# Forgetting attention's scores: two heads in the two halves of the array's rows, three products each, one worker for both heads

## The chip, the cores and the metric

The kernel runs on one core of a Trainium2 chip. Its engines are TensorE (matrix products; the profile writes PE, and PEld for its weight loads), VectorE (DVE), ScalarE (ACT), GpSimd (POOL) and SyncE (SP, which issues most transfers). The metric is the device time of one execution in microseconds (us).

## The reference, cut to what matters

One layer of a hybrid encoder block on 1024 frames of width 1024: a combined projection feeds eight retention heads and eight forgetting-attention heads of 64 each; then an output projection, cross attention to 256 memory tokens, and a SwiGLU. All in fp32. The part that changes is the scores of the forgetting attention:

```python
fq = rmsnorm(fq.reshape(B, T, N_FOX_HEADS, HEAD_DIM), g_fox_q[l])
fk = rmsnorm(fk.reshape(B, T, N_FOX_HEADS, HEAD_DIM), g_fox_k[l])
...
F = jnp.cumsum(log_f, axis=1).transpose(0, 2, 1)
qh = (q * (d ** -0.5)).transpose(0, 2, 1, 3)
for blk in range(T // Q_BLOCK):
    logits = jnp.einsum('bhqd,bhkd->bhqk', qh[:, :, q0:kend], kh[:, :, :kend])
    logits = logits + F[:, :, q0:kend, None] - F[:, :, None, :kend]
    logits = jnp.where(causal, logits, NEG_INF)
    p = jax.nn.softmax(logits, axis=-1)
    outs.append(jnp.einsum('bhqk,bhkd->bhqd', p, vh[:, :, :kend]))
```

## The kernel before

Every fp32 product is made of products of parts: an operand is split into a high part in fp32r (a reduced fp32 form that the array takes in one pass) and the remainder as a low part. The projections take three products (high by high, high by low, low by high).

The mixing stage goes through eight chunks of projection columns, four pairs of heads p = 0 to 3, retention and attention in turn: r0, f0, r1, f1, r2, f2, r3, f3. Then come the memory's keys and values (`kv_main`), W_out (`wout_main`), and the rest of the layer, which the change does not touch.

**The order.** TensorE's instruction order is written by a planner, class `Driver`. Each piece of work is a generator. It yields either a condition, or a pair (cost, delay): the cost moves the planner's clock `now` on, and the generator is not called again until `now` has passed the delay times `slow` (SLOW = 2.0 in the mixing stage, 1.8 from chunk r3's end on). Spawned generators go ahead of the main line; the main line (the projections) goes on where none is ready; if nothing is ready, the clock moves on with no instruction put down. The clock exists only while the kernel is written: on the chip TensorE takes the instructions in the order put down and waits at each for what it needs. `take_s` and `take_tp` reserve one of three `ps_s` banks or one of two `ps_tp` banks of PSUM for a planned while, `hold` times 1.5.

**The attention of a pair** (`fox_main`) waits until `fox_left` is 0, that is, until the workers of the pair before have finished; its tiles `kst`, `vst` and `fb` have one buffer each. The main line then makes eight projections of 384 columns, two a group, and for each of four groups g (two query tiles of 128 frames) spawns `prep`: three transposes a tile into a `ps_tp` bank, then evictions that leave the queries' high part twice over (128 rows: `qa`) and low part twice over (`qb`), and the keys' high part in rows 0 to 63 and low part in rows 64 to 127 of `kst`, for each head. So a product of 128 rows of `qa` with `kst` holds high by high and high by low at once, and `qb` with `kst` adds low by high and low by low.

Two workers, one a head, go through the groups in `fox_group`:
- scores: for each query tile n = 2g + i + 1 blocks of 128 keys in one or two pieces (`S_CUTS`), a piece being two products into one `ps_s` bank (L642, L643); VectorE adds the forget bias and keeps a running minimum while it reads the bank (L654); ScalarE takes the exponent with a row sum (L661) and scales by the reciprocal (L663), into `s_sb`, of which there are four buffers, two a worker;
- a pause (L665);
- values, for one worker at a time (token `pv`): transposes of `s_sb` in blocks of four into `ps_tp`, split into `p_hi` (ScalarE, L684) and `p_lo` (VectorE, L685), then four products with `vst` a block (L695, L696), and at the end, after the output is copied, a pause of 1200 ns times `slow` (L713).

The retention's scores (`ret_tile`, L463) are products of 64 rows, one head in rows 0 to 63, the other in 64 to 127, each written to its own bank, in plain fp32, which takes two instructions a product. `wout_main` starts when `h` exists, which `fox_end` makes once `fox_left` is 0 after the last pair.

Of the kernel before, what the change touches and what calls it, by code (L numbers as in the profile page):

```python
# [11 lines left out]
F32 = mybir.dt.float32  # L12
# [7 lines left out]
P = 128  # L20
D = 1024
T = 1024
# [131 lines left out]
def trace(tc, a, out):  # L154
# [463 lines left out]

    f_ready = [False]
    S_CUTS = {1: [1], 2: [2], 3: [3], 4: [4], 5: [3, 2], 6: [3, 3], 7: [4, 3], 8: [4, 4]}  # L620
    tok = {"s_sb": 2, "pv": 1}

    def fox_group(p, g, h, qa, qb, kst, vst, fb):

        yield lambda: tok["s_sb"] > 0
        tok["s_sb"] -= 1
        ptiles = []
        for i in range(2):
            qt = 2 * g + i
            n = qt + 1  # L630
            s_sb = foxp.tile([P, T], F32, name="s_sb", tag="s_sb", bufs=4)
            fd = foxp.tile([P, P], F32, name="fd", tag="fd", bufs=2)
            pol.affine_select(fd, fb[:, h, qt * P:(qt + 1) * P], [[-1, P]], ALU.is_ge, 1.0e30, base=0, channel_multiplier=1)
            mins = sm.tile([P, 4], F32, name="mins", tag="mins")
            nm = 0
            b0 = 0
            for nb in S_CUTS[n]:
                w = nb * P
                yield from take_s(1800)
                sps = ps_s()  # L640
                ks = kst[:, h, b0 * P:b0 * P + w]
                mm.matmul(sps[:, :w], qa[:, i, h, :], ks, start=True, stop=False)  # L642
                mm.matmul(sps[:, :w], qb[:, i, h, :], ks, start=False, stop=True)  # L643


                parts = []
                if b0 + nb == n:
                    if nb > 1:
                        parts.append((0, w - P, fb[:, h, b0 * P:b0 * P + w - P]))
                    parts.append((w - P, w, fd))  # L650
                else:
                    parts.append((0, w, fb[:, h, b0 * P:b0 * P + w]))
                for c0, c1, bias in parts:
                    dve.tensor_tensor_reduce(s_sb[:, b0 * P + c0:b0 * P + c1], sps[:, c0:c1], bias, 1.0,  # L654
                                             BIG if nm == 0 else mins[:, nm - 1:nm], ALU.add, ALU.min, mins[:, nm:nm + 1])
                    nm += 1
                b0 += nb
                yield 2 * max(w, 256) / 2.4, 0.0
            sums = sm.tile([P, 2], F32, name="sums", tag="sums")
            with prio(P_EXP):  # L660
                act.activation(s_sb[:, :n * P], s_sb[:, :n * P], AF.Exp, bias=mins[:, nm - 1:nm], scale=-1.0, accum_out=sums[:, 0:1])  # L661
                dve.reciprocal(sums[:, 1:2], sums[:, 0:1])
                act.activation(s_sb[:, :n * P], s_sb[:, :n * P], AF.Identity, scale=sums[:, 1:2])  # L663
            ptiles.append(s_sb)
# [24 lines left out]
        def products():  # L689
            jb, ph, pl, nu, at = blocks.pop(0)  # L690
            yield lambda: drv.now >= at
            for j, u0, cols in ((jb, 0, slice(0, 256)), (jb + 1, 2, slice(0, 256) if nu == 4 else slice(P, 256))):
                u1 = min(u0 + 2, nu)
                last = j == nj - 1
                mm.matmul(pv[:, cols], vst[:, h, j, :], ph[:, u0:u1, :], start=j == 0, stop=False, skip_group_check=True)  # L695
                mm.matmul(pv[:, cols], vst[:, h, j, :], pl[:, u0:u1, :], start=False, stop=last, skip_group_check=True)  # L696
            yield 4 * TR, 0.0

        for jb in range(0, nj, 2):
            yield from transposes(jb)  # L700
            if len(blocks) == 2:
                yield from products()
        tok["s_sb"] += 1
# [15 lines left out]
    def fox_main(c, p):  # L719
        w = weights.pop(c)  # L720
        yield lambda: fox_left[0] == 0
        fox_left[0] = 2
# [12 lines left out]
        drv.spawn(load_fb())  # L735
        parts = {}

        def worker(h):
            for g in range(NG):
                yield lambda: g in parts and fb_loaded[0]  # L740
                yield from fox_group(p, g, h, *parts[g], kst, vst, fb)
            fox_left[0] -= 1

        def prep(g, dups):
            yield 0.0, PREP
            qa = foxp.tile([P, 2, 2, P], F32R, name="qa", tag="qa", bufs=2)
            qb = foxp.tile([P, 2, 2, P], F32R, name="qb", tag="qb", bufs=2)
            for i in range(2):
                t = 2 * g + i
                yield from take_tp(2200)  # L750
                tp = ps_tp()
                for j in range(3):
                    flip(tp[:, j, :], dups[i][:, 2 * j:2 * j + 2, :].rearrange("p b d -> p (b d)"))
                cols = slice(t * P, (t + 1) * P)
                act.activation(qa[:, i], tp[:, 0:2, :], AF.Identity, scale=gqk[:, 0:1])
                for h in range(2):
                    r = slice(h * HD, (h + 1) * HD)
                    act.activation(kst[:HD, h, cols], tp[r, 2, :], AF.Identity, scale=gqk[r, 1:2])
                dve.scalar_tensor_tensor(qb[:, i], tp[:, 0:2, :], gqk[:, 0:1], f32(qa[:, i]), ALU.mult, ALU.subtract)
                for h in range(2):  # L760
                    r = slice(h * HD, (h + 1) * HD)
                    dve.scalar_tensor_tensor(kst[HD:, h, cols], tp[r, 2, :], gqk[r, 1:2], f32(kst[:HD, h, cols]), ALU.mult, ALU.subtract)
                yield 3 * TR, 0.0
            yield 0.0, 1600.0 + SLACK
            parts[g] = (qa, qb)

        drv.spawn(worker(0))
        drv.spawn(worker(1))
        for g in range(NG):
            fqk = foxp.tile([P, 2, 256], F32, name="fqk", tag="fqk", bufs=1)  # L770
            for i in range(2):
# [14 lines left out]
                load_chunk(c + 1)  # L786
            with prio(P_FQK):
                ss = sm.tile([P, 8], F32, name="ss8", tag="ss8")
                dups = [foxp.tile([P, 6, HD], F32, name="dup", tag="dup", bufs=2) for _ in range(2)]
                for i in range(2):  # L790
                    sq = dups[i][:, :4, :]
                    act.activation(sq.rearrange("p a d -> p (a d)"), fqk[:, i, :], AF.Square)
                    dve.tensor_reduce(ss[:, 4 * i:4 * i + 4], sq, AX.X, ALU.add)
                r = rstd(ss, 8, 1.0 / HD)
                for i in range(2):

                    x = fqk[:, i, :].rearrange("p (a d) -> p a d", d=HD)
                    q, k = r[:, 4 * i:4 * i + 2], r[:, 4 * i + 2:4 * i + 4]
                    pol.tensor_tensor(dups[i][:, :4, :].rearrange("p (a b) d -> p a b d", b=2), x[:, :2].unsqueeze(2).to_broadcast([P, 2, 2, HD]),
                                      q.unsqueeze(2).unsqueeze(3).to_broadcast([P, 2, 2, HD]), ALU.mult)  # L800
# [652 lines left out]
```

## Time and profile before

| | |
|---|---|
| time, median of three runs | 1608.91 us (1605.29 to 1613.33) |
| profiled execution, its time | 1609.22 us |
| its span, first to last instruction | 1607.5 us |
| TensorE busy in the span | 97% |
| VectorE, ScalarE, GpSimd busy | 62%, 47%, 10% |
| mean granted TensorE clock | 0.987 of 2.4 GHz |

A busy share is an average over the whole span. Durations of matrix products overlap, since the next one starts before the last has left the array: how fast they follow each other is read from one start to the next. The granted clock is the one that the chip gave TensorE, 1.0 for 2.4 GHz and 0.5 for 1.2.

### The profile page before, as it was taken

Reading aid. Unit: us, or ns where it says so; the run is one execution under the profiler, and the core shown is the slowest. Engines: PE = TensorE matmul, PEld = TensorE weight load, DVE = VectorE, ACT = ScalarE, POOL = GpSimd, SP = SyncE. Lnnn points to the kernel's source line nnn. Section 1 sums busy time; section 2 is a strip of 40 time slices with the busy share of each in tenths; the row PEclk is TensorE's granted clock in tenths of the full one; section 3 lists DMA queues with packets and bytes.
Section 4 is the critical chain, followed back from the end, with each engine's and each line's share of the span. In section 5 each row is a group of like instructions: output and inputs, shape, how many; then the busy total and the mean of one; then the engine's idle time right before and its main releaser. Section 6 shows DMA issues by size and latency. Waiting matters only on the chain.

```text
span 1607.5 us, 21839 instructions
## 1 busy us (share of the span) xinstructions
PE 1552.7 (97%) x7960; PEld 1311.5 (82%) x7960; DVE 995.0 (62%) x2050; ACT 751.8 (47%) x1621; POOL 155.2 (10%) x318
## 2 busy tenths in 40 slices
PE   7999999999999999999989969999999999899998
PEld 6997897898898878888878857888888888688887
DVE  6667657657668943455554567555555554599994
ACT  5457566557658841355554344333333333234231
POOL 0332222232232000000000000000000000000000
PEclk9999999999999999999999989999999999999999
DMA  7031121121133471200343404222222222571202
GB/s 227 6 89 47 35 64 47 35 61 49 35 103 100 137 239 53 79 1 33 104 140 105 119 27 121 89 79 79 79 80 79 79 79 85 217 273 61 96 0 106
DMA packets 142798, 142.15 MB, mean 88 GB/s; under 512 B 9049, under 2 KB 110681, under 8 KB 142178
## 3 DMA queue, kind: packets, MB, share of 16 engines
q1 hardware_dynamic: 138370, 125.02, 25.2%
q0 software_dynamic: 4320, 15.73, 2.5%
q8 instruction: 63, 1.03, 0.3%
q14 instruction: 45, 0.37, 0.1%
HBM read 112.38 MB, written 28.34 MB: 88 GB/s over the span
## 4 chain that ended last, share of the span: by engine, by line
PE 85%; DVE 5%; ACT 5%; DMA 2%; issue 2%; POOL 1%; SPq 0%; POOLq 0%; DVEq 0%; ACTq 0%
PE ps_mm L270 10%; PE ps_mm L271 10%; PE ps_mm L272 10%; PE ps_s L1167 7%; PE ps_s L1169 7%; PE ps_s L1168 7%; PE ps_tp L175 5%; PE ps_tp L1167 4%; PE ps_tp L1168 4%; PE ps_tp L1169 4%; PE ps_mm L1168 2%; PE ps_mm L1169 2%; PE ps_mm L1167 2%; PE ps_pv L696 1%; PE ps_s L270 1%
## 5 line engine op out<-in xcount | busy, mean ns | idle before, releaser
L270 PE MATMUL ps_mm<-w_hi,cv_hi 128*128 128x512 f32 x384 | 156.0, 406 | 6.3 <-ACT qsq L1081 3.3
L272 PE MATMUL ps_mm<-w_hi,cv_lo 128*128 128x512 f32 x384 | 152.3, 397 | 0.0
L271 PE MATMUL ps_mm<-w_lo,cv_hi 128*128 128x512 f32 x384 | 152.1, 396 | 0.0
L1332 ACT CAST op<-raw_d 128x2048 fp32r<-128x2048 f32 (+1 forms) x42 | 72.7, 1764 | 126.5 <-issue 50.8
L1290 ACT CAST w_hi<-t 128x512 fp32r<-128x512 f32 x88 | 54.2, 621 | 160.2 <-PE ps_tp L1168 71.8
L240 DVE TENSOR_TENSOR w_lo<-raw,w_hi 128x1024 fp32r<-128x1024 f32 (+2 forms) x75 | 88.2, 1181 | 29.4 <-ACT w_hi L239 28.1
L239 ACT CAST w_hi<-raw 128x1024 fp32r<-128x1024 f32 (+2 forms) x75 | 74.9, 1003 | 58.1 <-PE ps_mm L272 39.5
L1291 DVE TENSOR_TENSOR w_lo<-t,w_hi 128x512 fp32r<-128x512 f32 x88 | 60.3, 687 | 65.8 <-ACT w_hi L1290 65.8
L270 PE MATMUL ps_mm<-w_hi,hn_last 128*128 128x384 f32 (+2 forms) x256 | 96.7, 378 | 1.0 <-DVE t L291 1.0
L270 PE MATMUL ps_mm<-w_hi,hn_hi 128*128 128x384 f32 (+2 forms) x256 | 96.2, 376 | 0.1
L1333 DVE TENSOR_TENSOR op<-raw_d,op 128x2048 fp32r<-128x2048 f32 (+1 forms) x42 | 87.3, 2109 | 8.1 <-ACT op L1332 8.1
L271 PE MATMUL ps_mm<-w_lo,hn_hi 128*128 128x384 f32 (+2 forms) x256 | 91.0, 356 | 0.0
L270 PEld LDWEIGHTS ps_mm<-w_hi,cv_hi 128*128 128x128 f32 x384 | 73.1, 190 | 21.8 <-ACT qsq L1081 3.8
L272 PE MATMUL ps_mm<-w_hi,hn_lo 128*128 128x384 f32 (+2 forms) x256 | 90.8, 355 | 0.0
L272 PE MATMUL ps_mm<-w_hi,hn_last 128*128 128x384 f32 (+2 forms) x256 | 90.4, 353 | 0.0
L271 PE MATMUL ps_mm<-w_lo,hn_last 128*128 128x384 f32 (+2 forms) x256 | 90.1, 352 | 0.0
L272 PEld LDWEIGHTS ps_mm<-w_hi,cv_lo 128*128 128x128 f32 x384 | 73.1, 190 | 17.0
L271 PEld LDWEIGHTS ps_mm<-w_lo,cv_hi 128*128 128x128 f32 x384 | 73.3, 191 | 14.7
L1167 PE MATMUL ps_tp<-xQ,w_hi 128*128 128x512 f32 x176 | 70.8, 402 | 14.0 <-ACT w_hi L1290 14.0
L1290 ACT CAST w_hi<-raw_w 128x512 fp32r<-128x512 f32 x60 | 37.2, 621 | 89.5 <-PE ps_s L1168 85.6
L1168 PE MATMUL ps_tp<-xQ,w_hi 128*128 128x512 f32 x176 | 70.9, 403 | 0.0
L1169 PE MATMUL ps_tp<-xQ,w_lo 128*128 128x512 f32 x176 | 70.7, 402 | 0.0
(378 smaller groups left out, 4255.5 us busy)
## 6 DMA issues: line engine op xcount, KB each, us to landing
raw_w<-w_gate SPq DMA_DIRECT2D x44, 256.0 KB, 3.1
raw_w<-w_up SPq DMA_DIRECT2D x44, 256.0 KB, 4.3
a_dram<-at POOLq DMA_DIRECT2D x22, 512.0 KB, 2.9
raw<-w_in SPq DMA_DIRECT2D x32, 256.0 KB, 4.0
raw<-w_xkv SPq DMA_DIRECT2D x16, 512.0 KB, 3.8
of<-o_dram SPq DMA_DIRECT2D x16, 512.0 KB, 4.1
raw_d<-a_dram SPq DMA_DIRECT2D x8, 1024.0 KB, 5.3
raw_d<-w_down SPq DMA_DIRECT2D x8, 1024.0 KB, 6.0
```

The source lines that it names most:

```text
L175: flip = lambda o, x: mm.transpose(o, x, ident)
L239: act.copy(hi, raw)
L240: dve.tensor_tensor(lo, raw, f32(hi), ALU.subtract)
L270: mm.matmul(o, xh, wh, start=first, stop=False)
L271: mm.matmul(o, xh, wl, start=False, stop=False)
L272: mm.matmul(o, xl, wh, start=False, stop=last)
L1167: mm.matmul(q, wh, xh, start=first and k == 0, stop=False, skip_group_check=True)
L1168: mm.matmul(q, wh, xl, start=False, stop=False, skip_group_check=True)
L1169: mm.matmul(q, wl, xh, start=False, stop=k == n - 1, skip_group_check=True)
L1290: act.copy(hi, x)
L1332: act.copy(hi, x)
L1333: dve.tensor_tensor(lo, x, f32(hi), ALU.subtract)
```

## The change

`prep` makes two transposes a tile, for both tiles of a group in one `ps_tp` bank, and keeps queries and keys once: high and low parts in tiles of their own (`qh`, `ql`, `kst[:, 0]`, `kst[:, 1]`), head 0 in rows 0 to 63, head 1 in rows 64 to 127. A piece of scores is now six products of 64 rows into two `ps_s` banks, the two heads in turn: high by high, high by low, low by high; the product of the low parts is left out. Both heads' softmax follows. One worker goes through the groups: scores of both heads, the pause, the values of head 0, the values of head 1. `S_CUTS`, the pauses, `SLOW`, and the number of banks and of `s_sb` buffers stay. The diff without the lines that only move:

```diff
-    tok = {"s_sb": 2, "pv": 1}
-    def fox_group(p, g, h, qa, qb, kst, vst, fb):
-        yield lambda: tok["s_sb"] > 0
-        tok["s_sb"] -= 1
+    tok = {"pv": 1}
+    def fox_scores(g, qs, kst, fb):
+        rows = [slice(h * HD, (h + 1) * HD) for h in range(2)]
+        ptiles = [[], []]
         for i in range(2):
...
             for nb in S_CUTS[n]:
                 w = nb * P
                 yield from take_s(1800)
-                sps = ps_s()
-                ks = kst[:, h, b0 * P:b0 * P + w]
-                mm.matmul(sps[:, :w], qa[:, i, h, :], ks, start=True, stop=False)
-                mm.matmul(sps[:, :w], qb[:, i, h, :], ks, start=False, stop=True)
+                yield from take_s(1800)
+                sps = [ps_s(), ps_s()]
+                c = slice(b0 * P, b0 * P + w)
+                for m, (q, k) in enumerate(((0, 0), (0, 1), (1, 0))):
+                    for h, r in enumerate(rows):
+                        mm.matmul(sps[h][:, :w], qs[q][r, i, :], kst[r, k, c], start=m == 0, stop=m == 2)
...
-                yield 2 * max(w, 256) / 2.4, 0.0
+                yield 3 * max(w, 256) / 2.4, 0.0
...
-        yield 0.0, SMAX + n * 350.0 + SLACK
+        return ptiles
+
+    def fox_values(p, g, h, ptiles, vst):
         yield lambda: tok["pv"] > 0
...
-        def worker(h):
+        def worker():
             for g in range(NG):
                 yield lambda: g in parts and fb_loaded[0]
-                yield from fox_group(p, g, h, *parts[g], kst, vst, fb)
+                ptiles = yield from fox_scores(g, parts[g], kst, fb)
+                yield 0.0, SMAX + (2 * g + 2) * 350.0 + SLACK
+                for h in range(2):
+                    yield from fox_values(p, g, h, ptiles[h], vst)
             fox_left[0] -= 1
...
+            qh = foxp.tile([P, 2, P], F32R, name="qh", tag="qh", bufs=2)
+            ql = foxp.tile([P, 2, P], F32R, name="ql", tag="ql", bufs=2)
+            yield from take_tp(2200)
+            tp = ps_tp()
             for i in range(2):
-                t = 2 * g + i
-                yield from take_tp(2200)
-                tp = ps_tp()
-                for j in range(3):
-                    flip(tp[:, j, :], dups[i][:, 2 * j:2 * j + 2, :].rearrange("p b d -> p (b d)"))
...
+                for j in range(2):
+                    flip(tp[:, 2 * j + i, :], dups[i][:, 2 * j:2 * j + 2, :].rearrange("p b d -> p (b d)"))
...
+                act.activation(hi, src, AF.Identity, scale=gqk[:, j:j + 1])
+                dve.scalar_tensor_tensor(lo, src, gqk[:, j:j + 1], f32(hi), ALU.mult, ALU.subtract)
...
-        drv.spawn(worker(0))
-        drv.spawn(worker(1))
+        drv.spawn(worker())
...
-                    pol.tensor_tensor(dups[i][:, 4:, :], x[:, 2:], k.unsqueeze(2).to_broadcast([P, 2, HD]), ALU.mult)
+                    pol.tensor_tensor(dups[i], x, r[:, 4 * i:4 * i + 4].unsqueeze(2).to_broadcast([P, 4, HD]), ALU.mult)
```

## Rows read from the trace of the kernel before

**Rows 1.** The page: busy us (share of the span) x instructions, TensorE first.

```profile
PE 1552.7 (97%) x7960; PEld 1311.5 (82%) x7960; DVE 995.0 (62%) x2050; ACT 751.8 (47%) x1621; POOL 155.2 (10%) x318
```

**Rows 2.** By line, pairs 0 and 3: ns min/median/max, first and last start.

```profile
L642 PE MATMUL ps_s<-kst,qa x24: 222/338/423, 106.5 to 179.9; 128*128 128x384 f32 x10, 128*128 128x512 f32 x8, 128*128 128x256 f32 x4, 128*128 128x128 f32 x2
...
L696 PE MATMUL ps_pv<-p_lo,vst x40: 273/282/388, 118.7 to 202.2; 128*128 128x256 f32 x32, 128*128 128x128 f32 x8
...
L270 PE MATMUL ps_mm<-w_hi,hn_hi x64: 332/392/497, 206.9 to 287.4; 128*128 128x384 f32 x32, 128*128 128x512 f32 x32
...
L696 PE MATMUL ps_pv<-p_lo,vst x40: 272/281/415, 497.4 to 580.8; 128*128 128x256 f32 x32, 128*128 128x128 f32 x8
...
L270 PE MATMUL ps_mm<-w_hi,cv_hi x16: 389/389/443, 580.9 to 591.3; 128*128 128x512 f32 x16
```

**Rows 3.** Timeline of TensorE in pair 0: start, duration, line, operation, count.

```profile
106.71 0.33 PE L642 MATMUL ps_s<-kst,qa 128*128 128x256 f32 x1
...
114.88 0.49 PE L175 MATMUL ps_tp<-ident,s_sb 128*128 128x128 f32 x3
...
118.97 0.27 PE L696 MATMUL ps_pv<-p_lo,vst 128*128 128x128 f32 x1
...
121.88 0.34 PE L642 MATMUL ps_s<-kst,qa 128*128 128x384 f32 x1
...
164.76 0.39 PE L642 MATMUL ps_s<-kst,qa 128*128 128x512 f32 x1
...
168.28 0.39 PE L642 MATMUL ps_s<-kst,qa 128*128 128x512 f32 x1
...
181.66 1.04 PE L175 MATMUL ps_tp<-ident,s_sb 128*128 128x128 f32 x8
...
192.92 1.04 PE L175 MATMUL ps_tp<-ident,s_sb 128*128 128x128 f32 x8
...
202.18 0.28 PE L696 MATMUL ps_pv<-p_lo,vst 128*128 128x128 f32 x1
```

**Rows 4.** Timeline of TensorE around two visits to the half array (L463).

```profile
144.58 0.34 PE L642 MATMUL ps_s<-kst,qa 128*128 128x384 f32 x1
144.76 0.34 PE L643 MATMUL ps_s<-kst,qb 128*128 128x384 f32 x1
145.03 0.49 PE L463 MATMUL ps_s<-qT,kT 64*128 64x128 f32 x4
145.45 0.50 PE L270 MATMUL ps_mm<-w_hi,hn_hi 128*128 128x512 f32 x1
145.78 0.40 PE L271 MATMUL ps_mm<-w_lo,hn_hi 128*128 128x512 f32 x1
146.02 0.39 PE L272 MATMUL ps_mm<-w_hi,hn_lo 128*128 128x512 f32 x1
...
169.19 0.82 PE L463 MATMUL ps_s<-qT,kT 64*128 64x128 f32 x4 [0.28 <-DVE mins L654]
```

**Rows 5.** By line: score readings, exponent, scaling (from the timeline), low part.

```profile
L654 DVE CUSTOM_DVE_ANT_0 s_sb<-ps_s,fb x56: 272/553/689, 107.2 to 559.3; 128x384 f32<-128x384 f32 x24, 128x512 f32<-128x512 f32 x16, 128x128 f32<-128x128 f32 x8, 128x256 f32<-128x256 f32 x8
L654 DVE CUSTOM_DVE_ANT_0 s_sb<-ps_s,fd,mins x56: 339/346/352, 107.7 to 564.7; 128x128 f32<-128x128 f32 x56
L654 DVE CUSTOM_DVE_ANT_0 s_sb<-ps_s,fb,mins x32: 346/479/618, 143.8 to 562.9; 128x256 f32<-128x256 f32 x16, 128x128 f32<-128x128 f32 x8, 128x384 f32<-128x384 f32 x8
...
L661 ACT ACTIVATE s_sb<-s_sb,mins x64: 399/776/1155, 107.4 to 565.6; 128x128 f32<-128x128 f32 x8, 128x256 f32<-128x256 f32 x8, 128x384 f32<-128x384 f32 x8, 128x512 f32<-128x512 f32 x8
...
173.59 1.15 ACT L663 ACTIVATE s_sb<-s_sb,sums 128x1024 f32<-128x1024 f32 x1 [0.23 <-DVE sums L662]
...
L685 DVE TENSOR_TENSOR p_lo<-ps_tp,p_hi x80: 541/681/694, 118.1 to 578.6; 128x512 fp32r<-128x512 f32 x48, 128x384 fp32r<-128x384 f32 x32
```

**Rows 6.** Waits (us, times, longest), and a window: us, PE PEld DVE ACT POOL busy, PEclk.

```profile
PE ps_tp L175 <- DVE kst L762: 8.1, 5, 2.5
...
376.70:380.10 3.40, 3.40 (x10) 2.71 (x9) 3.34 (x15) 3.34 (x10) 0.29 (x1) 0.50 0.43 124
```

More of the change, by code (lines that the diff above doesn't have):

```diff
@@ L630, in fox_group @@
             n = qt + 1
[L631 to L634, printed above, removed]
+            s_sb = [foxp.tile([P, T], F32, name="s_sb", tag="s_sb", bufs=4) for _ in range(2)]
+            fd = [foxp.tile([P, P], F32, name="fd", tag="fd", bufs=2) for _ in range(2)]
+            mins = [sm.tile([P, 4], F32, name="mins", tag="mins", bufs=4) for _ in range(2)]
+            for h in range(2):
+                pol.affine_select(fd[h], fb[:, h, qt * P:(qt + 1) * P], [[-1, P]], ALU.is_ge, 1.0e30, base=0, channel_multiplier=1)
             nm = 0
@@ new lines, in fox_scores @@
+                for h in range(2):
+                    parts = []
+                    if b0 + nb == n:
+                        if nb > 1:
+                            parts.append((0, w - P, fb[:, h, b0 * P:b0 * P + w - P]))
+                        parts.append((w - P, w, fd[h]))
+                    else:
+                        parts.append((0, w, fb[:, h, b0 * P:b0 * P + w]))
+                    m = nm
+                    for c0, c1, bias in parts:
+                        dve.tensor_tensor_reduce(s_sb[h][:, b0 * P + c0:b0 * P + c1], sps[h][:, c0:c1], bias, 1.0,
+                                                 BIG if m == 0 else mins[h][:, m - 1:m], ALU.add, ALU.min, mins[h][:, m:m + 1])
+                        m += 1
@@ L657, in fox_group @@
+                nm = m
                 b0 += nb
-                yield 2 * max(w, 256) / 2.4, 0.0
-            sums = sm.tile([P, 2], F32, name="sums", tag="sums")
+                yield 3 * max(w, 256) / 2.4, 0.0
             with prio(P_EXP):
-                act.activation(s_sb[:, :n * P], s_sb[:, :n * P], AF.Exp, bias=mins[:, nm - 1:nm], scale=-1.0, accum_out=sums[:, 0:1])
-                dve.reciprocal(sums[:, 1:2], sums[:, 0:1])
-                act.activation(s_sb[:, :n * P], s_sb[:, :n * P], AF.Identity, scale=sums[:, 1:2])
@@ L664, in fox_group @@
-            ptiles.append(s_sb)
-        yield 0.0, SMAX + n * 350.0 + SLACK
+                for h in range(2):
+                    sums = sm.tile([P, 2], F32, name="sums", tag="sums", bufs=4)
+                    act.activation(s_sb[h][:, :n * P], s_sb[h][:, :n * P], AF.Exp, bias=mins[h][:, nm - 1:nm], scale=-1.0, accum_out=sums[:, 0:1])
+                    dve.reciprocal(sums[:, 1:2], sums[:, 0:1])
+                    act.activation(s_sb[h][:, :n * P], s_sb[h][:, :n * P], AF.Identity, scale=sums[:, 1:2])
+                    ptiles[h].append(s_sb[h])
@@ L721, in fox_main @@
         yield lambda: fox_left[0] == 0
-        fox_left[0] = 2
+        fox_left[0] = 1
         kst = foxp.tile([P, 2, T], F32R, name="kst", tag="kst", bufs=1)
@@ L736, in fox_main @@
         parts = {}
-        def worker(h):
+        def worker():
             for g in range(NG):
                 yield lambda: g in parts and fb_loaded[0]
-                yield from fox_group(p, g, h, *parts[g], kst, vst, fb)
+                ptiles = yield from fox_scores(g, parts[g], kst, fb)
+                yield 0.0, SMAX + (2 * g + 2) * 350.0 + SLACK
+                for h in range(2):
+                    yield from fox_values(p, g, h, ptiles[h], vst)
             fox_left[0] -= 1
@@ L745, in prep @@
             yield 0.0, PREP
[L746 to L747 removed]
+            qh = foxp.tile([P, 2, P], F32R, name="qh", tag="qh", bufs=2)
+            ql = foxp.tile([P, 2, P], F32R, name="ql", tag="ql", bufs=2)
+            yield from take_tp(2200)
+            tp = ps_tp()
             for i in range(2):
[L749 to L763 removed]
+                for j in range(2):
+                    flip(tp[:, 2 * j + i, :], dups[i][:, 2 * j:2 * j + 2, :].rearrange("p b d -> p (b d)"))
+            cols = slice(2 * g * P, (2 * g + 2) * P)
+            for j, hi, lo in ((0, qh.rearrange("p i t -> p (i t)"), ql.rearrange("p i t -> p (i t)")), (1, kst[:, 0, cols], kst[:, 1, cols])):
+                src = tp[:, 2 * j:2 * j + 2, :].rearrange("p i t -> p (i t)")
+                act.activation(hi, src, AF.Identity, scale=gqk[:, j:j + 1])
+                dve.scalar_tensor_tensor(lo, src, gqk[:, j:j + 1], f32(hi), ALU.mult, ALU.subtract)
+            yield 4 * TR, 0.0
             yield 0.0, 1600.0 + SLACK
[L765 to L768 removed]
+            parts[g] = (qh, ql)
+        drv.spawn(worker())
         for g in range(NG):
@@ L788, in fox_main @@
                 ss = sm.tile([P, 8], F32, name="ss8", tag="ss8")
-                dups = [foxp.tile([P, 6, HD], F32, name="dup", tag="dup", bufs=2) for _ in range(2)]
+                dups = [foxp.tile([P, 4, HD], F32, name="dup", tag="dup", bufs=2) for _ in range(2)]
                 for i in range(2):
-                    sq = dups[i][:, :4, :]
+                    sq = dups[i]
                     act.activation(sq.rearrange("p a d -> p (a d)"), fqk[:, i, :], AF.Square)
```

16 lines of the change are left out of this document (removed).

## The prediction

> **What bounds the kernel now.** Read the page first [rows 1]: TensorE is busy for 1552.7 of 1607.5 us. So the sum is made on TensorE's instruction stream, and a saving on ScalarE or VectorE counts only where TensorE waits for it. The stream is written out in order by the planner, so what matters beside the instructions is where the order leaves TensorE nothing to do.
>
> Next, one line at a time inside one pair's stretch [rows 2]. The attention of pair 0 runs from its first score at 106.5 us to its last value product at 202.2 us, and the projection of the next attention chunk, which may not start before `fox_left` is 0, starts at 206.9 us. In pair 3 the last value product stands at 580.8 us and W_out's first product, which has to wait for the same, at 580.9. The attention of a pair is thus a chain of some 96 us that ends just ahead of what waits for it (4.7 us for pair 0, of which the planned pause behind the last product takes 2.4 or more). The reader is to keep this: two heads in two workers fill the time that a pair has, with about 2 us to spare.
>
> Then the order of events inside that chain, as a timeline [rows 3], and the waits [rows 6].
>
> **The arithmetic on TensorE.** Before, a head's piece of scores is two products of 128 rows, after, three of 64 rows for both heads. A 384-column product takes 0.18 us from start to start (144.58 to 144.76), a 512-column one 0.23 to 0.24 (145.78 to 146.02) [rows 4]; for 256 columns I take 0.12 and for 128 columns 0.11, an estimate by columns (for 128, bounded by the next weight load). Per pair there are 12 pieces: one of 128 columns, two of 256, five of 384, four of 512. Before: 48 pieces of each head's kind, 96 in all, two products each, 34.0 us. After, if the two heads' products run at the same time: 48 x 3 steps, 25.8 us; if one behind the other, 51.5 us. The trace has no 64-row product in fp32r; the nearest row is the retention's L463 in fp32. There four instructions of the two heads, issued together, last 0.49 us from the first start to the last end (145.03); where the second head came late the same four last 0.82 us (169.19) [rows 4]. So halves of the array overlap, and I take 25.8 us, keeping 51.5 as the other end (+25.8 on the sum).
>
> Each visit to the half-array form has a price in the same rows: from L643 at 144.76 to L463 it is 0.27 us where a 384-column step is 0.18, and behind it the first 512-column product takes 0.33 us where 0.23 is usual. That is 0.19 us a visit, 48 visits, 9.2 us; the bounds are 0 (pieces back to back) and 9.2, and I take 9.2 as most pieces stand alone between projections. So the scores come out at 35.0 against 34.0 us: +1.0.
>
> Here a rule of the Trainium skill stands against the row. TensorEngine Tiling (Array Packing), Theoretical Speedup, gives up to 2x for a contraction of 64; by it alone the scores fall by 8.2 us and the kernel gains. The same page's Key Properties say that a change of tiling mode drains the engine; the 0.19 us above agrees with that, and takes the 8.2 us back. The sum by the table alone would be lower by 9.2 us than mine.
>
> `prep` loses two of six transposes a group, 32 in all, at 0.11 us (eight at 181.66 last 1.04 us with the last one's 0.27 in it [rows 3]): -3.5 us. Its evictions on ScalarE and VectorE shrink, and it takes one ps_tp tile where it took two. TensorE waited 8.1 us for that tile in five places [rows 6]; with a tile left free I take all of it back, bounds 0 and -8.1. Behind one of these waits the granted clock is 0.50, the 1.2 GHz level, from 376.7 to 380.1 us [rows 6], which loses 1.7 us. TensorE's work alone thus says -3.5 + 1.0 - 8.1 - 1.7, about -12 us.
>
> **The order.** This is the term that decides. `worker` becomes one generator for both heads. Its steps a group: scores of both heads, the pause, values of head 0, its closing pause, values of head 1, its closing pause, next group. Nothing of one head stands beside the other's pause any more. From [rows 3], for one head of pair 0:
> - scores to first transposes: group 0, 106.71 to 114.88, 8.2 us; group 3, 168.28 to 181.66, 13.4 us (13.0 for head 1). The pauses in the code are (1750 + 350(2g + 2) + 1000) ns times SLOW = 2: 6.9, 8.3, 9.7 and 11.1 us, so planned time stretches by 1.1 to 1.2 on the chip. Four groups: 36.0 planned, 39 to 41 us.
> - values, with the closing pause: group 0, 114.88 to the next group's score at 121.88, 7.0 us, of which the pause behind the last product is 2.9 (118.97 to 121.88); group 3, 192.92 to 202.18 plus 2.9, 12.2 us. With groups 1 and 2 estimated between them (7.0, 7.5, 9.5, 12), some 36 us a head, 71 for two.
> - scores: a piece now takes two of three ps_s banks at once. In [rows 3] three pieces go together from 164.76 and the fourth waits until 168.28, 3.5 us. Two banks a time gives about 3.3, 3.6, 8 and 8.5 us for the groups, 23 us.
>
> Before, the two workers share these pauses: 40 + 36 + 12 + waits for the one value bank = 96, as measured. After: 40 + 71 + 23 = 134 us if there were projections enough to fill it. There are not. Between 106.5 and 206.9 us TensorE has 100.4 us, of which the attention itself is some 28 (8.5 scores; 72 transposes at 0.11, 7.9; 64 value products of 256 columns at 0.12 and 16 of 128 at 0.09, 9.1; 2 in `prep`), some 2 are waits and 70 are projections and retention. With the attention's work of three groups between them (20 us) and 2 us of waits those 70 us are used up about 92 us after the first score. The chain then stands at 15 (scores of three groups) + 27 (their pauses) + 48 (their values) = 90: the last group's scores are about to begin. From there TensorE has only this group, and the time is that of VectorE and ScalarE.
>
> That tail, from the readings and softmax of one head [rows 5]: VectorE reads the scores of one head in 0.69 + 0.48 + 0.35 + 0.69 + 0.62 + 0.35 us (pieces of 512, 256 + 128, 512, 384 + 128 columns), 6.4 us for both, about 8 us in with the accumulator reads between them and the first piece. ScalarE has exponent and scaling of 896 columns for two heads (1.05 us each, by 0.108 us less than 1024 columns take: 1155 less 399 ns over seven steps of 128), also until about 8 us in, then 1024 columns (1.16 + 1.15) for head 0: the first transposes are at 10.7 us. Head 1's softmax holds ScalarE until 13.4. From there a block of four transposes costs 0.44 us, ScalarE's copy (about as long as VectorE's part) and 0.68 us on VectorE (L685) to its first product, and 0.68 us for each further one; four blocks of two heads end at 22 to 23 us. TensorE works some 9.5 us of that. So the next chunk starts 92 + 22.5 = 114.5 us after the first score, not 100.4: +14 us, less 2 us of retention's last pieces that then stand in the gap: +12 a pair. Pair 3 has pauses of 1.8 for 2.0, no retention, and W_out behind it: +10. In each tail there is a stop of about 5 us between the scores and the first transposes, longer than the 2.5 us at most behind which the clock halved, so 1.7 us more each, or twice that.
>
> Sum: 3 x 12 + 10 = 46, clock +7, and of the -12 us only what is not TensorE work under the chain: a pair is now set by its chain, so the clock regained near 376 us and what stands ahead of the first score count, about -4. Together +49. Where the tail starts is known to the nearest piece of scores only, 3.3 us, and projections can reach into it; I take 2 us off each of the four, -8: +41. The profiled execution took 1609.2 us, 1.7 more than its span, and is the median of the runs (1608.9) within 0.3. Predicted: 1650 us.
>
> **Rivals.**
> The halves do not overlap in fp32r. For: no row shows it. Against: L463 in [rows 4]. The pair's scores cost 6.4 us more, of which 58% (groups 0 to 2) lengthens the filler's cover and the rest the tail, mostly behind VectorE: about +2.5 us a pair on top, 1660. (Without the long chain it would give 1609 + 25.8 - 12 = 1623.)
>
> Faster: the next chunk is not held back, because the chain keeps within the about 2 us that pair 0 has to spare. Then the arithmetic stands alone: 1609 - 3.5 + 1.0 - 8.1 - 1.7 = 1597. It decides if both heads' values follow each other without the pauses of [rows 3] between them. Against it: those pauses are in the generator and were in the stream before.
>
> Even: the projections last longer than I count, or the tail's work is done while they last, so that a tail costs 3 us and the -12 us pay for it: 1609. For: the softmax of head 0 in group 3 stood ready at 174.7 us and its transposes came at 181.66 [rows 3, 5], so the stream's pauses are longer than the work.
>
> **Chances.** Forecast 0.66, no overlap with the long chain 0.16, faster 0.09, even 0.09. About 0.5% (8 us) is what a measurement tells from no change. Slower 0.82, same 0.09, faster 0.09. A tail of 7 to 18 us more a pair gives 1633 to 1680 in the forecast's own case; the range goes down to 1612, where the shortest tails meet the even case, which leaves about 2 in 10 outside.
>
> **What the profile after would show.** Right: the time from a pair's first score to the next chunk's first projection is 110 to 118 us, not 100; ahead of it a stretch of 15 us or more with only transposes and value products on TensorE, with waits on ScalarE's and VectorE's p_hi, p_lo and s_sb; granted clock 0.50 behind some of them; 64-row products of two heads starting within 0.01 us; the wait of L175 on `kst` gone. Wrong: projections in between the last group's values, and a chunk start near 100 us after the first score; or six steps a piece where I count three.

## The result and the profile after

| | before | after |
|---|---|---|
| time, median of four runs each | 1607.10 us (1604.06 to 1613.33) | 1674.19 us (1673.04 to 1675.46) |
| span of the profiled execution | 1607.5 us | 1671.3 us |
| mean granted TensorE clock | 0.987 | 0.970 |

The ratio is 1.0416, 95% interval 1.0389 to 1.0442: slower by 67 us, where 41 were forecast. The same line of the page after, beside [rows 1]:

```profile
PE 1578.9 (94%) x8024; PEld 1318.8 (79%) x8024; DVE 970.2 (58%) x1986; ACT 728.8 (44%) x1557; POOL 141.9 (8%) x286
```

TensorE has 64 products more and is busy 26 us longer; VectorE, ScalarE and GpSimd do less. The span grew by 64 us, so most of the loss is time in which TensorE has nothing to do. Where, the lines of pairs 0 and 3 say, beside [rows 2] (first and last start at the end of each count):

```profile
L646 PE MATMUL ps_s<-kst,qh x48: 271/392/504, 104.7 to 205.3; 64*128 64x384 f32 x20, 64*128 64x512 f32 x16, 64*128 64x256 f32 x8, 64*128 64x128 f32 x4
...
L706 PE MATMUL ps_pv<-p_lo,vst x40: 274/282/579, 119.6 to 225.3; 128*128 128x256 f32 x32, 128*128 128x128 f32 x8
...
L270 PE MATMUL ps_mm<-w_hi,hn_hi x64: 332/388/498, 225.4 to 293.5; 128*128 128x384 f32 x32, 128*128 128x512 f32 x32
...
L270 PE MATMUL ps_mm<-w_hi,cv_hi x72: 389/394/447, 650.7 to 699.8; 128*128 128x512 f32 x72
```

The next chunk's first projection comes 0.1 us behind the pair's last value product, 120.7 us after the pair's first score; before it was 100.4. From one attention chunk's first projection to the next (to W_out's first product for the last) the trace of after has 147.0, 143.5, 147.7 and 134.1 us, that of before 126.8, 124.8, 126.2 and 123.0: +71.4 in all. Behind W_out's first product the span is 5.9 us shorter than before, where TensorE had waited 3.0 us for `h` until 595 us, and the chunks start 1.7 us earlier; 71.4 - 5.9 - 1.7 = 63.8 is the difference of the spans. The wait for `h`, in the kernel before:

```profile
595.17 0.80 PE L270 MATMUL ps_mm<-w_hi,cv_hi 128*128 128x512 f32 x1 [3.01 <-DVE h L838]
```

The end of pair 0 on TensorE's timeline (start, duration, line, operation, count; in brackets the idle time before it and what ended it):

```profile
190.41 0.39 PE L272 MATMUL ps_mm<-w_hi,hn_last 128*128 128x512 f32 x1
190.64 0.60 PE L175 MATMUL ps_tp<-ident,s_sb 128*128 128x128 f32 x4
...
195.10 0.52 PE L175 MATMUL ps_tp<-ident,s_sb 128*128 128x128 f32 x3 [3.17 <-DVE p_lo L695]
...
199.67 0.93 PE L646 MATMUL ps_s<-kst,qh 64*128 64x512 f32 x4
...
201.43 0.61 PE L646 MATMUL ps_s<-kst,qh 64*128 64x384 f32 x3 [0.60 <-DVE mins L659]
...
203.40 0.70 PE L646 MATMUL ps_s<-kst,qh 64*128 64x512 f32 x3 [0.87 <-DVE mins L659]
...
208.40 0.28 PE L175 MATMUL ps_tp<-ident,s_sb 128*128 128x128 f32 x1
211.92 1.75 PE L175 MATMUL ps_tp<-ident,s_sb 128*128 128x128 f32 x7 [3.24 <-ACT s_sb L670]
...
225.30 0.27 PE L706 MATMUL ps_pv<-p_lo,vst 128*128 128x128 f32 x1
225.41 0.39 PE L270 MATMUL ps_mm<-w_hi,hn_hi 128*128 128x384 f32 x1
```

The last projection starts at 190.41 us. For 35 us TensorE then has only attention and the retention's last pieces, and it stands idle behind VectorE's `p_lo`, behind the score readings and behind ScalarE's softmax. The stretch ahead of this tail, the four tails, and the whole stage from the first attention chunk to W_out (window, its length, busy us of PE, PEld, DVE, ACT, POOL, then the granted clock):

```profile
86.00:190.40 104.40, 103.49 (x604) 87.41 (x604) 56.94 (x208) 52.55 (x153) 26.61 (x57) 1.00 0.16 45
190.40:225.40 35.00, 24.55 (x137) 19.69 (x136) 21.67 (x68) 20.57 (x45) 8.26 (x14) 0.80 0.29 86
334.30:368.90 34.60, 24.52 (x138) 19.64 (x136) 21.65 (x68) 20.57 (x45) 8.27 (x14) 0.80 0.30 88
477.60:516.60 39.00, 27.34 (x146) 22.66 (x145) 22.70 (x73) 21.98 (x50) 7.29 (x14) 0.74 0.28 91
616.40:650.70 34.30, 22.73 (x116) 16.87 (x114) 19.00 (x48) 19.08 (x30) 0.56 (x2) 0.70 0.29 82
...
78.40:650.70 572.30, 518.67 (x2924) 440.04 (x2921) 324.40 (x1056) 311.96 (x787) 109.03 (x223) 0.94 0.22 66
```

The same stage of the kernel before:

```profile
80.10:580.90 500.80, 488.01 (x2859) 429.39 (x2858) 344.75 (x1116) 331.05 (x848) 122.32 (x255) 0.99 0.24 70
```

So of the +71.5 us between these two windows, 40.8 are idle time (53.6 less 12.8) and 30.7 are longer busy time, much of it at the half clock: in the 104 us ahead of the first tail the granted clock is 1.00, in the tails 0.70 to 0.80.

The waits that stand in the place of the one in [rows 6] (us, times, longest); the wait on `kst` is gone:

```profile
PE ps_tp L175 <- ACT s_sb L670: 13.5, 4, 4.0
PE ps_s L646 <- DVE mins L659: 10.6, 13, 1.4
PE ps_s L463 <- DVE mins L659: 8.2, 7, 1.2
PE ps_tp L175 <- DVE p_lo L695: 7.3, 4, 3.2
```

And a visit to the half-array form among projections, beside [rows 4]:

```profile
158.59 0.39 PE L271 MATMUL ps_mm<-w_lo,hn_last 128*128 128x512 f32 x1
158.82 0.40 PE L272 MATMUL ps_mm<-w_hi,hn_last 128*128 128x512 f32 x1
159.15 0.62 PE L646 MATMUL ps_s<-kst,qh 64*128 64x384 f32 x4
159.59 0.34 PE L646 MATMUL ps_s<-kst,ql 64*128 64x384 f32 x2
159.87 0.50 PE L270 MATMUL ps_mm<-w_hi,hn_last 128*128 128x512 f32 x1
160.21 0.39 PE L271 MATMUL ps_mm<-w_lo,hn_last 128*128 128x512 f32 x1
```

Six products of 384 columns, three for each head, take 0.72 us, and the two heads' products start within 0.01 us of each other: the heads share their time. The visit as a whole is to be read from 158.82 to 160.21, 1.39 us. Two 512-column steps of 0.23 and three 384-column steps of 0.18 are 1.00 of that; the change of form and back costs the other 0.39: 0.10 on the way in, 0.19 inside, 0.11 behind it. Of eight visits of this width that stand alone between two 512-column projections at the full clock, seven take 1.38 to 1.39 us; a visit of 128-column products costs 0.34 by the same reading.

### The profile page after: what moved, and what is told of

Same layout as the page of the kernel before. It is cut to its first block, busy times and chain, and to the rows that moved or that the text cites. A ratio compares the mean times of both kernels' runs of the same rounds, so it can differ in the third digit from the quotient of the medians.

```text
span 1671.3 us, 21824 instructions
## 1 busy us (share of the span) xinstructions
PE 1578.9 (94%) x8024; PEld 1318.8 (79%) x8024; DVE 970.2 (58%) x1986; ACT 728.8 (44%) x1557; POOL 141.9 (8%) x286
## 4 chain that ended last, share of the span: by engine, by line
PE 86%; DVE 5%; ACT 4%; DMA 3%; issue 2%; SPq 0%; POOL 0%; DVEq 0%; POOLq 0%; ACTq 0%
PE ps_mm L270 11%; PE ps_mm L272 11%; PE ps_mm L271 11%; PE ps_s L1170 6%; PE ps_s L1171 6%; PE ps_s L1172 6%; PE ps_tp L175 4%; PE ps_tp L1170 4%; PE ps_tp L1172 4%; PE ps_tp L1171 4%; PE ps_mm L1171 2%; PE ps_mm L1172 2%; PE ps_mm L1170 2%; PE ps_s L646 2%; PE ps_pv L706 1%
## 5 line engine op out<-in xcount | busy, mean ns | idle before, releaser
L1293 ACT CAST w_hi<-t 128x512 fp32r<-128x512 f32 x88 | 54.2, 621 | 159.3 <-PE ps_tp L1171 71.5
```

Source lines behind the costliest of these rows:

```text
L1293: act.copy(hi, x)
```

## The experiments

All kernels with the changed form leave out the product of the low parts, as the change does. "Stage" is the stretch from the first attention chunk's first projection to W_out's first product; busy and clock are TensorE's there. The first row is the kernel before, as above.

| kernel | time, us | ratio to before (95%) | stage, us | busy | clock |
|---|---|---|---|---|---|
| before | 1607 | | 500.8 | 488.0 | 0.99 |
| the change | 1674.2 | 1.0416 (1.0389 to 1.0442) | 572.3 | 518.7 | 0.94 |
| order alone | 1696.0 | 1.0556 (1.0527 to 1.0585) | 594.6 | 529.7 | 0.94 |
| form alone, heads apart | 1617.5 | 1.0065 (1.0044 to 1.0085) | 515.2 | 511.3 | 1.00 |
| head by head | 1668.9 | 1.0377 (1.0360 to 1.0393) | 566.7 | 519.6 | 0.95 |
| no closing pause | 1647.2 | 1.0245 (1.0228 to 1.0263) | 544.1 | 502.0 | 0.97 |
| half the pause | 1655.0 | 1.0294 (1.0274 to 1.0314) | 556.0 | 510.2 | 0.95 |
| pipelined | 1626.9 | 1.0123 (1.0092 to 1.0154) | 528.4 | 503.2 | 0.97 |
| pipelined, form before | 1629.6 | 1.0136 (1.0103 to 1.0168) | 529.4 | 497.2 | 0.98 |
| pipelined, banks together | 1635.0 | 1.0167 (1.0152 to 1.0183) | 534.9 | 508.4 | 0.98 |
| pipelined, half the pause | 1626.4 | 1.0104 (1.0087 to 1.0121) | 526.2 | 497.2 | 0.98 |
| pipelined, both | 1604.9 | 0.9979 (0.9967 to 0.9992) | 505.7 | 492.7 | 1.00 |
| both, banks reserved shorter | 1610.3 | 1.0018 (1.0004 to 1.0033) | 511.7 | 495.1 | 0.99 |
| before, joint preparation | 1606.0 | 0.9985 (0.9975 to 0.9996) | 498.6 | 483.2 | 1.00 |

**Order or form.** Two theories: the one worker's longer chain ("order"), or the half-array products ("form"). First the order alone, on the products and the preparation of before:

```diff
-        def worker(h):
+        def worker():
...
-                yield from fox_group(p, g, h, *parts[g], kst, vst, fb)
+                ptiles = []
+                for h in range(2):
+                    ptiles.append((yield from fox_scores(g, h, *parts[g], kst, fb)))
+                yield 0.0, SMAX + (2 * g + 2) * 350.0 + SLACK
+                for h in range(2):
+                    yield from fox_values(p, g, h, ptiles[h], vst)
```

> The kernel before with one thing changed: one worker for both heads (scores of head 0, scores of head 1, the pause, values of head 0, values of head 1); its 128-row products, its prep and its transposes stay. Order theory (the single chain is longer than the projections that cover it, and its uncovered end costs the time): 1655 to 1685 us, near the changed kernel's 1674, with the next chunk's first projection 115 to 125 us after a pair's first score. Form theory (the rival: the half-array products, with their change of mode and two banks a piece, cost the time): 1600 to 1615 us, as before.

Then the form and the preparation of after, with the heads apart in two workers:

```diff
-                yield from take_s(1800)
-                sps = [ps_s(), ps_s()]
+                sps = ps_s()
...
-                    for h, r in enumerate(rows):
-                        mm.matmul(sps[h][:, :w], qs[q][r, i, :], kst[r, k, c], start=m == 0, stop=m == 2)
+                    mm.matmul(sps[:, :w], qs[q][r, i, :], kst[r, k, c], start=m == 0, stop=m == 2)
...
-        drv.spawn(worker())
+        drv.spawn(worker(0))
+        drv.spawn(worker(1))
```

> The changed kernel with two workers again, one a head, each taking its own three 64-row products alone into one bank; prep and its tiles as in the changed kernel, the product of the low parts left out as there. Order theory: the chain is covered as before, and only TensorE's arithmetic counts: 51.5 us of steps and 96 visits at 0.19 us, 18, against 34.0, less 3.5 and up to 10 of the waits in prep: 1607 + 36 - 4 to -13 = 1630 to 1639 us, 1620 to 1645 with scatter. Form theory: twice the visits of the changed kernel, so 1674 us or more.

The order alone costs 89 us, more than the whole change and more than the theory gave; from the first score of pairs 0 to 2 to the next chunk it takes 123.5, 129.0 and 133.8 us. There the pieces of head 1 follow those of head 0, so it is not quite the order of the change; why it costs more was not tried. The form alone costs 10, less than its own range of 1620 to 1645: the heads share time in a few of the first pieces only, and TensorE's stage is busy for 511.3 us, but some 50 visits to the form stand in the trace where 96 were priced. The two costs do not add up to 67, so neither is the exact share of its part. But with the order the loss is there on either form, and without it all but 10 us stay away: the order is the cause.

**Do the halves share their time?** Only the order of the six products is changed:

```diff
-                for m, (q, k) in enumerate(((0, 0), (0, 1), (1, 0))):
-                    for h, r in enumerate(rows):
+                for h, r in enumerate(rows):
+                    for m, (q, k) in enumerate(((0, 0), (0, 1), (1, 0))):
```

> The changed kernel; the only edit is that of each score piece head 0's three products are issued, then head 1's three, instead of in turn. Theory 'the halves of the array run at once only as neighbours in the queue': only the product at the seam shares its time, so a step goes from three products of length to about five, 25.8 us of streams become 43, +17 us of which the part beside projections counts fully and the part in the tails too: 1684 to 1695. Rival 'the halves never shared time, the step is short for another reason' or 'the queue looks ahead far enough': 1671 to 1678, and steps of the same length (0.72 us for 384 columns).

It came out at 1668.9 us, below both ranges and not slower than the change (the intervals of the two ratios just meet): the theory of neighbours falls. In its timeline the visit that answers to 159.15 above reads:

```profile
160.92 0.62 PE L646 MATMUL ps_s<-kst,qh 64*128 64x384 f32 x4
161.37 0.35 PE L646 MATMUL ps_s<-kst,ql 64*128 64x384 f32 x2
161.64 0.50 PE L270 MATMUL ps_mm<-w_hi,hn_last 128*128 128x512 f32 x1
```

The program now has two `qh`, one `ql`, two `qh`, one `ql`; the chip started all four `qh` before either `ql`, and the six took the same 0.72 us. The second half's products did not wait for those of the first that stood ahead of them. The section on the kernel before says that TensorE takes the instructions in the order put down; between the two halves of the array it did not do so here. That six products take the time of three is what the Trainium skill says in TensorEngine Tiling (Array Packing), Key Properties: tiles run their loads and products in parallel. The trace agrees.

**Which part of the order.** The worker's fixed pauses, one kind at a time. The pause behind each head's values (1200 ns, doubled by `SLOW`) no longer holds the worker up, and the value bank is asked for at its first product:

```diff
-        yield 0.0, 1200.0
-        tok["pv"] += 1
+        def release():
+            yield 0.0, 1200.0
+            tok["pv"] += 1
+        drv.spawn(release())
```

> The changed kernel; the only edit is that the planner's pause of 1200 (stretched to 2.4 us) behind each head's values no longer holds up the worker, and that the accumulator's bank is asked for at the first value product. 8 such pauses are 19 us of a pair's chain. Theory 'order' (the pairs are longer because one worker's chain with its pauses is longer than the projections that cover it): the uncovered tail of 35 us a pair shrinks by some 8 to 15 us, 1620 to 1650. Rival 'products' (what is lost are PE's own waits on banks and readings of the side by side products, and these pauses are covered): 1668 to 1680.

And the pause between scores and values is halved:

```diff
-                yield 0.0, SMAX + (2 * g + 2) * 350.0 + SLACK
+                yield 0.0, 0.5 * (SMAX + (2 * g + 2) * 350.0 + SLACK)
```

> The changed kernel; the only edit is that the planner's pause between a group's scores and its values is halved (36 us a pair in planner time become 18). Theory 'the pause itself is the chain's length': the pair's chain is up to 18 us shorter, 1615 to 1645. Rival 'exponentials really are that late': PE then waits for the score rows at the first transposes as long as it was spared before, 1668 to 1685, and the wait of the transposes on the rows grows from 13.5 us to over 40.

They give back 27 and 19 us; the second lies between the two ranges. Halving the pause did not raise the transposes' wait on `s_sb` in all (13.8 us in seven places for 13.5 in four), so the half taken away was mostly not time that the softmax needed; the scores' wait on their banks grew (14.4 us for 10.6).

**The chain taken apart.** Each head's values become a generator of their own that takes its turn, and the next group's scores start as soon as both heads' transposes have freed the `s_sb` buffers:

```diff
+                yield lambda: tok["s_sb"] == 2
+                tok["s_sb"] -= 2
                 ptiles = yield from fox_scores(g, parts[g], kst, fb)
-                yield 0.0, SMAX + (2 * g + 2) * 350.0 + SLACK
                 for h in range(2):
-                    yield from fox_values(p, g, h, ptiles[h], vst)
+                    drv.spawn(fox_values(p, g, h, ptiles[h], vst))
```

The edit is larger than these lines. Each head's pause now runs inside its own generator; the value bank is asked for at the first product and the closing pause no longer holds up the next head, as in the run without the closing pause; and at most two blocks of `p_hi` and `p_lo` are under way.

> The changed kernel's prep and its six 64-row products a piece, side by side, but the chain taken apart: the values of each head are a piece of work of their own, head 1's transposes follow head 0's at once, the value bank is asked for only at the first product, and the next group's scores begin when the transposes have freed the score tiles. Order theory: the chain fits in the projections again, 1595 to 1612 us; a pair's first score to the next chunk 98 to 104 us. Form theory: 1660 us or more, since every product and bank of the changed kernel is there.

The same order on the products and preparation of before:

> The same order as the pipelined kernel, with the 128-row products, prep and duplicated queries of the kernel before. Order theory: 1600 to 1614 us; what the pipelined half-array kernel is below this is the arithmetic of the form, by my sum +1.0 of scores, -3.5 of transposes and 0 to -10 of waits in prep: 3 to 12 us. Form theory: about 1607 us, and the pipelined half-array kernel 50 us or more above it.

47 of the 67 us come back, less than the order theory gave, and the two forms stop 3 us apart. So the loss that came back was the order's on either form. What is left is alike in size, but not in its longest waits (first two lines the changed form, third the form before):

```profile
PE ps_s L646 <- DVE mins L659: 7.5, 6, 1.9
PE ps_s L475 <- DVE mins L659: 4.6, 3, 2.0
...
PE ps_tp L175 <- DVE p_lo L690: 10.4, 13, 2.4
```

With the form before a piece takes one score bank; that the rest has one cause in both was not shown. With the changed form each two-head piece takes two of three score banks, which the retention (L463, L475) needs as well. With both banks taken in one moment, the second reserved for longer:

```diff
-                yield from take_s(1800)
-                yield from take_s(1800)
+                yield from take_two(1800, 2600)
...
+    def take_two(*holds):
+        sl = drv.slots.setdefault("s", [0.0] * NS)
+        yield lambda: sum(t <= drv.now for t in sl) >= 2
+        for hold in holds:
+            sl[sl.index(min(sl))] = drv.now + hold * HOLD
```

> The pipelined order with the changed form (1626.87), with one edit: the planner takes both score banks of a piece in one moment, and reserves the second head's for 2600 instead of 1800, so that no piece is issued right behind another whose bank is still read. Theory 'banks': of the 18 us by which its score steps exceed their streams 8 to 14 go, 1612 to 1620. Rival 'the rest is PE standing idle at the pair's end and its clock': within 4 us of it, 1623 to 1631.

The waits of the scores on their banks went (7.5 us to none listed), and the kernel became 8 us slower, above either range: a tail is back in each pair, as it would be if pieces that come later lengthen the chain. In pair 0:

```profile
200.70:218.20 17.50, 13.75 (x98) 12.27 (x97) 12.84 (x32) 9.67 (x25) 5.19 (x7) 0.90 0.46 122
```

The halved pause on the pipelined order, with the same edit as above:

> The pipelined order with the changed form (1626.87), with the planner's pause between a group's scores and its values halved as well. Theory 'the chain of a pair is still what is long': 1608 to 1618. Rival 'the pair now ends with the other projections, which stand still for the retention's chain, and that waits for score banks': the chain no longer sets the end and a shorter one gives nothing, 1622 to 1632.

Nothing, as the rival had it, and this time the scores waited:

```profile
PE ps_s L646 <- DVE mins L659: 11.6, 8, 1.8
PE ps_tp L175 <- ACT s_sb L670: 7.9, 4, 2.7
PE ps_s L475 <- DVE mins L659: 5.6, 3, 2.0
```

If either edit only moved the loss to where the other would have taken it, both at once should remove it. Then both with shorter reserves:

> The pipelined order with the changed form, both of the last two edits at once: banks taken together (alone 1634.96: no bank waits, but a tail of 17 us a pair) and the pause between scores and values halved (alone 1626.39: no tail, but 22 us of score steps above their streams). Theory 'each of the two left the other's loss': the bank waits stay gone and the tail goes, 1606 to 1618. Rival 'the two are one loss seen from two sides, since a two-head piece takes two of three banks': 1622 to 1636, with the waits back in another place.

> As the run before it, with the banks reserved for 1400 and 2000 instead of 1800 and 2600. Theory 'each left the other's loss': within 6 of that run, 1604 to 1620. Rival 'one loss seen from two sides': less reserved is more waited, 1620 to 1632, with the waits for the banks grown again.

Both at once gave 1604.94 us, ratio 0.9979 (0.9967 to 0.9992), 22 us less than the pipelined order alone and just under the theory's range: all 67 us are back, with the change's form, its preparation and its three score banks. Its page, the window of its stage, and the end of pair 0 on its timeline:

```profile
PE 1553.8 (97%) x8024; PEld 1294.0 (81%) x8024; DVE 970.5 (60%) x1986; ACT 724.8 (45%) x1557; POOL 143.0 (9%) x286
```

```profile
79.80:585.50 505.70, 492.65 (x2924) 414.98 (x2923) 319.75 (x1052) 304.39 (x784) 110.16 (x223) 1.00 0.24 69
```

```profile
202.47 0.27 PE L721 MATMUL ps_pv<-p_lo,vst 128*128 128x128 f32 x1
202.58 0.45 PE L270 MATMUL ps_mm<-w_hi,hn_last 128*128 128x512 f32 x1
...
209.08 0.33 PE L270 MATMUL ps_mm<-w_hi,hn_hi 128*128 128x384 f32 x1
```

The last value product of pair 0 now stands 6.6 us ahead of the next chunk, with projections behind it, and the clock is 1.00. With shorter reserves it is 5 us slower, within the theory's range; the waits for the banks did not grow, but the transposes' wait on `s_sb` is 13.4 us where it was 7.7. The last order was not tried on the form before.

**The preparation by itself,** on the kernel before: the transposes of two tiles go into two banks (four of queries, two of keys), and the copies are 512 and 256 columns wide, half as many:

```diff
+            yield from take_tp(2200)
+            tp = ps_tp()
             for i in range(2):
-                t = 2 * g + i
-                yield from take_tp(2200)
-                tp = ps_tp()
-                for j in range(3):
...
+                for j in range(2):
...
+            act.activation(flat(qa), src, AF.Identity, scale=gqk[:, 0:1])
+            dve.scalar_tensor_tensor(flat(qb), src, gqk[:, 0:1], f32(flat(qa)), ALU.mult, ALU.subtract)
...
+            yield from take_tp(2200)
+            tp = ps_tp()
+            for i in range(2):
+                flip(tp[:, i, :], dups[i][:, 4:6, :].rearrange("p b d -> p (b d)"))
```

> The kernel before, with its 128-row products, its two workers and its queries held twice; the only edit is that the transposes of a group's two tiles go into two banks (four of queries, two of keys) and their copies are made 512 and 256 columns wide, half as many. Theory 'the wait for kst in the old preparation was worth what it showed' (8.1 us of waiting and 1.7 us of the clock behind it): 1595 to 1602. Rival 'that time comes back elsewhere': 1604 to 1610.

2.7 us, not 10. The wait on `kst` is gone, and others stand in its place:

```profile
PE ps_s L642 <- DVE mins L654: 4.7, 6, 1.1
...
PE ps_tp L175 <- DVE qb L756: 2.7, 3, 1.1
PE ps_tp L175 <- ACT s_sb L663: 2.1, 1, 2.1
```

Its stage has 15.4 us of idle TensorE (498.60 less 483.15) where before had 12.8:

```profile
78.20:576.80 498.60, 483.15 (x2858) 425.93 (x2857) 333.39 (x1068) 318.21 (x800) 127.58 (x255) 1.00 0.24 71
```

## Why the prediction came out as it did

**The mechanism held.** One worker's chain outlasts the projections, and the next chunk waits for it. The first score to the next chunk was to be 110 to 118 us and was 120.7, 121.4 and 125.6 in pairs 0 to 2, a little over; the tail without projections, the waits on `p_lo` and `s_sb` and the half clock are there. The order alone reproduces the loss, and another order removes it. The time lay in the range (1674, where the forecast's own case went from 1633 to 1680), but the forecast was 24 us low, and three of its terms were mis-sized.

**Where the tail starts.** The projections were to be used up 92 us after the first score, with the last group's scores about to begin. They ended after 85.7 (104.72 to 190.41), and the last group's scores came 95.0 us after the first: 9.3 us in which group 2's second head and the retention's last pieces stood on TensorE alone. The last group itself took 25.7 us (199.67 to 225.41) for 22.5. So the tail is 35 and not 22.5 us, and a pair +20.2, +18.7 and +21.5, not +12; pair 3 +11.1 for +10. The caution of -8 for tails that projections reach into had the wrong sign.

**The clock, +7.** A stop behind the scores and 1.7 us behind it was the idea. The kernel with both edits has the same 2924 products in the stage and is busy 492.65 us at a clock of 1.00; the change is busy 518.67 at 0.94. That is 26 us more for the same work: the tails of 35 us have many short stops, and by the clocks of their four windows some 69 of 143 us were granted the lower level, 1.2 GHz (an estimate: twice each window's length times what its clock lacks to 1.00). Idle time makes the other 40.6 us between these two kernels. These 26 us are inside the pairs' +71.4; without them the pairs lost 45, near the 46 of the sum. (This cuts the same time another way than the tails above.) That it comes so near is partly luck, since the 46 rest on a tail of 22.5 us that begins as the projections run out, and neither was so. In the sum's own terms the miss is mostly the clock, 26 for 7, and the caution of -8.

**The arithmetic, -12.** Two terms of it were wrong, and the long chain hid that. The visit to the half-array form was priced at 0.19 us, from what it adds ahead of the products and behind them; the 0.19 to 0.20 inside was left out. [Rows 4] had it: L463 takes 0.42 us to the next start (145.03 to 145.45) for two steps of 128 columns, 0.22 by the prediction's own 0.11. With 0.39 us, taken for each, 48 visits are 18.7 us, and the scores come out at 44.5. The 34.0 of before is a little low as well: at the durations by which 144 steps are 25.8 us, 192 are 34.4. So it is about +10, not +1.0. Two kernels whose clock is 1.00 in this stage say nearly the same: both edits 492.65, before with joint preparation 483.15, +9.5, where an estimate of 10.1 less the 3.5 of the transposes is 6.6; the other 2.9 are not explained. And most of the 8.1 us of waits on `kst` did not come back: without them the kernel before gained 2.7. So the form saves nothing on TensorE here. In the pipelined order, on which both forms were run, TensorE's stage is 6 us busier with the changed form (at clocks of 0.97 and 0.98), and the kernel 2.7 us faster, which is what the joint preparation gave by itself. The kernel with both edits has a stage 4.9 us longer than before, and is ahead only because some 6.4 us behind W_out's first product, with the wait on `h`, are gone there as well; why that wait goes was not tried.

The rule on a drain at each change of mode (the Trainium skill, TensorEngine Tiling (Array Packing), Key Properties) was rightly weighed against the twofold speed of the same page, but at half its price. The trace agrees in that each visit costs time beside its products, 0.39 us; that the array is drained meanwhile cannot be seen in it.

**The rivals.** No overlap: refuted, six products in the time of three. Faster and even: neither was the change's, and the condition of the first, that the values of both heads follow without the pauses between them, is what the last order meets; it ends at 1605 and not at 1597. With the two wrong terms above put right, its sum would be 1609 - 3.5 + 10.1 - 2.7 = 1613, and 1607 with the 6.4 us taken off that it had left out behind W_out's first product (an estimate).

## What to carry to other kernels

When two generators that covered each other's pauses become one, add up the pauses along the new chain and set them against the work that can fill it, before counting products; the answer decided 89 us here, the products some 10. Price a change of the array's form from the last start before it to the second start behind it, as part of the cost sits inside and on both sides: 0.39 us here, where reading the two sides alone gave 0.19. And where removing a wait makes a kernel no faster, try it together with the edit that failed for the opposite reason: banks taken together cost 8 us, half the pause gave 0, both gave 22.

## What the runs showed that was not expected

The order of products for the two halves made no difference to a visit: issued three and three, they still ran in pairs, 0.72 us for six of 384 columns either way. And the lower clock cost 26 us beside 40.6 us of idle time: over tails of 34 to 39 us with 10 to 12 us of idle time each, in many short stops, the mean granted clock was 0.70 to 0.80.
